# Whole-group x transfers, a new order of transfers and an earlier table load in a matmul with bias and residual

## The chip, the core and the metric

The kernel runs on one core of a Trainium2 chip. A core has five engines that work side by side, each with an instruction queue of its own: TensorE (PE) for matrix products, VectorE (DVE), ScalarE (ACT), GpSimd (POOL) and SyncE (SP). SP computes nothing here. It issues the transfers (DMAs) between the chip's main memory and the on-chip memory, and each transfer is spread over 16 DMA engines. The engines keep step by semaphores: an instruction waits until a counter has reached a value.

The metric is the device time of one execution in microseconds (us). The median of three runs before the change is 210.46 us, the lowest 210.41 and the highest 210.52.

## The reference

```python
batch, m, k, n = 16, 512, 1024, 768
# x: [16, 512, 1024], weight: [1024, 768], bias: [768], residual: [16, 512, 768], all float32
return (np.matmul(x, weight) + bias + residual).astype(np.float32)
```

The sixteen batches are one matrix of 8192 rows. x has 33.6 MB, the residual and the output 25.2 MB each, the weight 3.1 MB.

## The kernel before

The 8192 rows are cut into 8 groups of 1024 rows. Within a group each of the 128 partitions holds 8 consecutive rows, so a partition's share of x is 8 rows of 4 KB, 32 KB that lie together in main memory; its share of the residual and of the output is 24 KB that lie together. The program handles x in halves of 4 rows a partition (B = 4), that is 16 halves. "Row tile" below means the 128 rows that have the same place j (0 to 7) in all partitions.

One large tile, `data`, holds everything that SP moves: four slots for residuals, which also become the output (the sum is formed in place and stored from there), and two slots for x, used by even and odd groups in turn. Two exceptions: the weight is first loaded over the fourth residual slot and what follows it, and the residual of group 7 lies in the x slot of the even groups (`r_home`).

The steps of one half:

- ACT (lines 122 to 132) waits for the half of x and casts it to bf16 in two pieces (`cast_x`, line 114), then copies half of the transposed blocks from `tq` to their place in `xt` (`move_blocks`, line 119, 8 copies). The semaphore of the first halves is `xa`, that of the second halves `xb`; each half adds 16, and the waited value rises by 16 each group. The semaphore `cast` counts the casts, four per group.
- DVE (lines 150 to 172) transposes the 32x32 blocks: `tq` from the first cast piece (line 136), `xt` directly from the second (line 142). Between those it adds the product in PSUM to the residual (`evacuate`, line 148), two row tiles at a time: those of places 0 and 2 in the second half of the same group, those of 4 and 6 in the first half of the next. Before its loop it clears `bias_rows` (line 150), waits for the bias to land (line 152) and spreads it over the partitions (line 153). Nothing on DVE's queue passes that wait.
- PE (lines 260 to 284) waits for the weight's cast (`wc`), then does for each half 4 row tiles of 8 pairs of matmuls, 128x512 and 128x256.
- POOL (lines 182 to 204) casts the weight in two parts, then adds the bias in place to two row tiles at a time (line 190).

SP walks through `ORDER` (line 216). Each name is one transfer: `x3a` and `x3b` the halves of group 3, `r3` its residual, `st3` its store, `st4+` the store of groups 4 and 5 together, `st7a` to `st7c` parts of the last store, `w0` and `w1` the halves of the weight. Waits in front of a transfer hold up all that stand behind it on SP: x of group 2 and later waits until the group two before it is cast (its slot is then free); a transfer of the kind `xa`, `xb` or `r` waits until the one before it of that kind has landed; r4 to r6 wait until the store four groups before has landed, r7 until group 6 is cast; a store waits until POOL has added the bias, the last one until DVE is done; the bias waits until DVE has cleared its tile.

```python
ORDER = ("x0a w0 w1 bias x0b r0 x1a x1b r1 x2a x2b r2 x3a x3b r3 x4a x4b st0 st1 r4 x5a x5b r5 "
         "st2 x6a x6b r6 x7a x7b r7 st3 st4+ st6 st7a st7b st7c ").split()
```

ACT's program also holds an instruction that the source doesn't show: a load of its function table, which the compiler places in front of the first cast, inside the loop over groups.

Of the kernel before, what the change touches and what calls it, by code (L numbers as in the profile page):

```python
# [7 lines left out]
FP32 = mybir.dt.float32  # L8
BF16 = mybir.dt.bfloat16
U32 = mybir.dt.uint32  # L10
P = 128
Q = 32
G = 8
B = 4

ORDER = ("x0a w0 w1 bias x0b r0 x1a x1b r1 x2a x2b r2 x3a x3b r3 x4a x4b st0 st1 r4 x5a x5b r5 "
         "st2 x6a x6b r6 x7a x7b r7 st3 st4+ st6 st7a st7b st7c ").split()
PARTS = {"": (0, 8), "a": (0, 4), "b": (4, 8)}
LAST_PARTS = {"a": (0, 4), "b": (4, 6), "c": (6, 8)}


@with_exitstack
def kernel(
    ctx: ExitStack,
    tc: tile.TileContext,
    x: bass.AP,
    weight: bass.AP,
    bias: bass.AP,
    residual: bass.AP,
    out: bass.AP,  # L30
):
    nc = tc.nc
    with tc.tile_critical(name="all", no_gpsimd_drain=True), ExitStack() as es:  # L33
        emit(nc, es, x, weight, bias, residual, out)


def emit(nc, es, x, weight, bias, residual, out):
    x2d = x.flatten_outer_dims()
    res2d = residual.flatten_outer_dims()
    out2d = out.flatten_outer_dims()  # L40
    M, K = x2d.shape
    N = weight.shape[1]
    R = K // P
    KH = K // 2
    n_sub = M // P
    n_grp = n_sub // G
    n_bat = n_sub // B
    chunks = [(0, 512), (512, N - 512)]
    sp, act, dve, pool, pe = nc.sync, nc.scalar, nc.vector, nc.gpsimd, nc.tensor

    def sbuf(name, shape, dtype):
        return es.enter_context(nc.sbuf_tensor(name, shape, dtype))

    R_SLOT, X_SLOT = G * N, G * K
    X1, X0 = 4 * R_SLOT, 4 * R_SLOT + X_SLOT
# [2 lines left out]
    bias_rows = sbuf("bias_rows", [P, N], FP32)  # L58
    bias_bc = sbuf("bias_bc", [P, N], FP32)
    xb = sbuf("xb", [P, 2, B, R // 2, 2 * Q, 2], BF16)  # L60
    tq = sbuf("tq", [P, B, R // 2, 2, Q], U32)
    xt = sbuf("xt", [P, 2, B, R // 2, P], U32)
    po = es.enter_context(nc.psum_tensor("po", [P, 4, 1024], FP32))
# [3 lines left out]
    def sem(name):  # L67
        if name not in sems:
            sems[name] = es.enter_context(nc.semaphore(name))
        return sems[name]  # L70

    def wait(eng, name, value):
        eng.wait_ge(sem(name), value)
# [14 lines left out]
    def group(ap, g):  # L88
        return ap[g * G * P:(g + 1) * G * P, :].rearrange("(p j) k -> p j k", p=P)

    def span(start, size):
        return data[:, start:start + size] if isinstance(start, int) else data[:, bass.ds(start, size)]

    def x_half(g, half):
        return span(X0 - (g % 2) * X_SLOT + half * (B * K), B * K).rearrange("p (t k) -> p t k", k=K)

    def r_home(g):

        return (g % 4) * R_SLOT + ((g + 1) // n_grp) * (X0 - 3 * R_SLOT)

    def r_rows(start, j, n):
        return span(start + j * N, n * N).rearrange("p (j n) -> p j n", n=N)
# [7 lines left out]


    def cast_x(g, half, c):
        part = x_half(g, half)[:, :, c * KH:(c + 1) * KH]
        act.copy(out=xb[:, c],  # L114
                 in_=part.rearrange("p t (a j r) -> p t j a r", j=R // 2, r=2)).then_inc(sem("cast"), 1)

    def move_blocks(half, q):
        for m in range(P // Q):
            act.copy(out=xt[q * Q:(q + 1) * Q, half, :, :, m * Q:(m + 1) * Q],  # L119
                     in_=tq[m * Q:(m + 1) * Q, :, :, q]).then_inc(sem("mv"), 1)  # L120

    xa, xo = Rising(act, "xa", 16, 16), Rising(act, "xb", 16, 16)
    tm, tqs = Rising(act, "tm", 1, 1), Rising(act, "tq", 1, 1)
    with act.Fori(0, n_grp) as g:  # L124
        for half, loaded in ((0, xa), (1, xo)):
            loaded.wait()
            cast_x(g, half, 0)
            tm.wait()
            cast_x(g, half, 1)
            tqs.wait()  # L130
            for q in (0, 1):
                move_blocks(half, q)
# [49 lines left out]
    for h in (0, 1):  # L182
        part = slice(h * (R // 2), (h + 1) * (R // 2))
# [24 lines left out]
    def load_into(name):  # L208

        before = landed.get(name, 0)  # L210
        landed[name] = before + 16
        if before:
            wait(sp, name, before)
        return name

    for name in ORDER:
        into = name
        if name == "bias":
            wait(sp, "ev", EV0)
            src, dst = bias[None, :].to_broadcast((P // Q, N)), bias_rows[0:P:Q, :]  # L220
        elif name[0] == "w":
            k0 = int(name[1]) * (R // 2)
            src, dst = w_rows[:, k0:k0 + R // 2, :], w_stage[:, k0:k0 + R // 2, :]
        elif name[0] == "x":
            g, part = int(name[1]), name[2:]
            j0, j1 = PARTS[part]
            if g > 1 and part == "a":
                wait(sp, "cast", 2 * (2 * g - 2))
            if g == 3 and part == "a":
                wait(sp, "wc", 2)  # L230
            into = load_into(name[0] + part)
            src, dst = group(x2d, g)[:, j0:j1, :], x_half(g, j0 // B)
        elif name[0] == "r":
            g = int(name[1])
            if g == n_grp - 1:
                wait(sp, "cast", 2 * (2 * g))
            elif g > 3:
                wait(sp, f"st{g - 4}", 16)
            into = load_into("r")
            src, dst = group(res2d, g), r_rows(r_home(g), 0, G)  # L240
        else:
            g, part = int(name[2]), name[3:]
            n = 2 if part == "+" else 1
            j0, j1 = (LAST_PARTS if g == n_grp - 1 else PARTS)[part.strip("+")]
            end = (g + n - 1) * G + j1
            if end == n_sub:
                wait(sp, "ev", ev_end)
            else:
                wait(sp, "add", added[end - 1])
            src, dst = r_rows(r_home(g), j0, j1 - j0), group(out2d, g)[:, j0:j1, :]  # L250
            if n > 1:
                src = span(r_home(g), n * R_SLOT).rearrange("p (g k) -> p g k", g=n)
                dst = out2d[g * G * P:(g + n) * G * P, :].rearrange(
                    "(g p j) n -> p g (j n)", g=n, p=P)
            if g > 2:
                into, stored = "st", stored + 16
        sp.dma_start(out=dst, in_=src).then_inc(sem(into), 16)
# [4 lines left out]
    with pe.Fori(0, n_bat) as b:  # L262
        mv.wait()
        tm.wait()
        for i in range(B):
# [4 lines left out]
            for k in range(R):  # L270
                lhsT = words[:, k // 2, k % 2, :]
                for c, (n0, nl) in enumerate(chunks):
                    dst, rhs = po[:, i, n0:n0 + nl], w_sb[:, k, n0:n0 + nl]
                    if c == 0:
                        ins = pe.matmul(dst, lhsT=lhsT, rhs=rhs, start=(k == 0), stop=(k == R - 1))  # L275
                    else:
                        ins = pe.add_instruction(mybir.InstMatmult(  # L277
                            name=nc.get_next_instruction_name(),
# [34 lines left out]
```

## Time and profile before

| | before |
|---|---|
| median of 3 runs | 210.46 us (210.41 to 210.52) |
| the profiled execution, its own time | 210.49 us |
| its span, first to last instruction | 208.7 us |
| PE busy | 170.1 us, 82% of the span |
| DVE busy | 166.3 us, 80% |
| ACT busy | 154.0 us, 74% |
| POOL busy | 115.5 us, 55% |
| DMA packets' time, share of 16 engines' span | 97.9% |
| bytes moved | 87.05 MB, mean 417 GB/s |

The span is what the profile shows; the profiled execution's own time is 1.8 us longer, since it includes what lies before the first and after the last instruction. "Share of 16 engines' span" adds the time of all DMA packets and divides by 16 times the span. A packet is one contiguous run that a DMA engine moves, or the 4 bytes with which it raises a semaphore at the end of its part of a transfer. The trace holds a record of each packet: start, duration and bytes.

By the trace's packet records the first packet starts at 2.2 us. Fifteen of the sixteen DMA engines end between 205.2 and 205.8 us and one ends at 207.2 us with the same bytes (5.44 MB).

### The profile page before, as it was taken

Reading aid. Unit: us, or ns where it says so; the run is one execution under the profiler, and the core shown is the slowest. Engines: PE = TensorE matmul, PEld = TensorE weight load, DVE = VectorE, ACT = ScalarE, POOL = GpSimd, SP = SyncE. Lnnn points to the kernel's source line nnn. Section 1 sums busy time; section 2 is a strip of 40 time slices with the busy share of each in tenths; the row PEclk is TensorE's granted clock in tenths of the full one; section 3 lists DMA queues with packets and bytes.
Section 4 is the critical chain, followed back from the end, with each engine's and each line's share of the span. In section 5 each row is a group of like instructions: output and inputs, shape, how many; then the busy total and the mean of one; then the engine's idle time right before and its main releaser. Section 6 shows DMA issues by size and latency. Waiting matters only on the chain.

```text
span 208.7 us, 2836 instructions
## 1 busy us (share of the span) xinstructions
PE 170.1 (82%) x1024; PEld 50.5 (24%) x512; DVE 166.3 (80%) x180; ACT 154.0 (74%) x168; POOL 115.5 (55%) x38
## 2 busy tenths in 40 slices
PE   0000399999999999999999999999999999999800
PEld 0000123332332233323322333233323222223200
DVE  1009686899989998999899989998999899983500
ACT  0365997697989799979997998889897989720000
POOL 0055002918484757566665757484839392999700
PEclk9999999999999999999999999999999999999965
DMA  6999999999999999999999999999999999999993
GB/s 207 433 427 455 414 427 446 454 404 408 449 415 436 443 414 436 443 447 391 443 443 405 451 410 447 413 436 430 429 429 446 429 405 452 443 424 410 436 415 139
DMA packets 5176, 87.05 MB, mean 417 GB/s; under 512 B 564, under 2 KB 564, under 8 KB 824
## 3 DMA queue, kind: packets, MB, share of 16 engines
q1 hardware_dynamic: 5176, 87.05, 97.9%
HBM read 61.88 MB, written 25.17 MB: 417 GB/s over the span
## 4 chain that ended last, share of the span: by engine, by line
DVE 30%; ACT 22%; issue 16%; DMA 15%; PE 10%; ACTq 1%; DVEq 1%; SPq 0%
DVE xt L142 17%; DMA data<-in_x_dram 15%; ACT xt L119 12%; ACT xb L114 8%; DVE tq L136 7%; PE po L275 7%; DVE data L148 6%; PE po L277 3%; ACT L114 2%; DVEq L84 1%; ACTq L84 0%; ACTq L114 0%; ACTq L124 0%; DVEq L148 0%; SPq L308 0%
## 5 line engine op out<-in xcount | busy, mean ns | idle before, releaser
L275 PE MATMUL po<-w_sb,xt 128*128 128x512 bf16 x512 | 169.2, 383 | 27.1 <-DVE xt L142 24.1
L190 POOL TENSOR_TENSOR data<-data,bias_bc 128x1536 f32<-128x1536 f32 x32 | 109.8, 3454 | 68.9 <-DVE data L148 68.7
L277 PE MATMUL po<-w_sb,xt 128*128 128x256 bf16 x512 | 140.6, 275 | 0.0
L119 ACT COPY xt<-tq 32x512 uint32<-32x512 uint32 x128 | 78.9, 617 | 20.1 <-DVE tq L136 17.3
L142 DVE STREAM_TRANSPOSE xt<-xb 32x512 uint32<-32x512 uint32 x128 | 90.2, 704 | 2.7 <-ACT xb L114 0.7
L275 PEld LDWEIGHTS po<-w_sb,xt 128*128 x512 | 50.5, 99 | 146.3 <-issue 144.4
L148 DVE TENSOR_TENSOR data<-po,data 128x1536 f32 (+2 forms) x33 | 56.0, 1709 | 12.4 <-PE po L277 11.9
L114 ACT CAST xb<-data 128x2048 bf16 x32 | 64.9, 2077 | 0.3
L136 DVE STREAM_TRANSPOSE tq<-xb 128x1024 uint32<-128x1024 uint32 x16 | 19.8, 1235 | 1.6 <-ACT xb L114 1.6
L114 ACT ACT_TABLE_LOAD x8 | 10.3, 1283 | 9.8 <-DMA data<-in_x_dram 9.6
L185 POOL CAST w_sb<-data 128x3072 bf16<-128x3072 f32 x2 | 5.5, 2744 | 12.8 <-DMA data<-in_weight_dram 12.8
L153 DVE LOAD_MASK_SELECT bias_bc<-bias_rows x1 | 0.0, 14 | 14.0 <-DMA bias_rows<-in_bias_dram 14.0
L150 DVE MEMSET bias_rows<- 128x768 f32 x1 | 0.7, 698 | 1.2 <-SPq L33 1.2
L153 DVE STREAM_SHUFFLE bias_bc<-bias_rows 128x768 f32<-128x768 f32 x1 | 1.0, 1005 | 0.0
L297 POOL MEMSET const-float32-0.0<- 128x1 f32 x1 | 0.1, 98 | 0.2 <-issue 0.2
L297 POOL MEMSET const-bfloat16-1.0<- 128x1 bf16 x1 | 0.1, 101 | 0.0
L297 POOL MEMSET const-uint8-127<- 128x1 uint8 x1 | 0.1, 101 | 0.0
L297 POOL MEMSET const-float32-1.0<- 128x1 f32 x1 | 0.1, 98 | 0.0
## 6 DMA issues: line engine op xcount, KB each, us to landing
data<-in_x_dram SPq DMA_DIRECT2D x16, 2048.0 KB, 17.1
data<-in_residual_dram SPq DMA_DIRECT2D x8, 3072.0 KB, 17.1
out_dram<-data SPq DMA_DIRECT2D x5, 3072.0 KB, 23.9
out_dram<-data SPq DMA_DIRECT2D x1, 6144.0 KB, 31.1
data<-in_weight_dram SPq DMA_DIRECT2D x2, 1536.0 KB, 12.3
out_dram<-data SPq DMA_DIRECT2D x1, 1536.0 KB, 10.1
out_dram<-data SPq DMA_DIRECT2D x2, 768.0 KB, 8.6
bias_rows<-in_bias_dram SPq DMA_DIRECT2D x1, 12.0 KB
```

The lines of the kernel that those rows point to most:

```text
L84: self.eng.reg_add(self.reg, self.reg, self.step)
L114: act.copy(out=xb[:, c], in_=part.rearrange("p t (a j r) -> p t j a r", j=R // 2, r=2)).then_inc(sem("cast"), 1)
L119: act.copy(out=xt[q * Q:(q + 1) * Q, half, :, :, m * Q:(m + 1) * Q], in_=tq[m * Q:(m + 1) * Q, :, :, q]).then_inc(sem("mv"), 1)
L136: dve.transpose(out=tq[:], in_=xb_words(0)).then_inc(sem("tq"), 1)
L142: ins = dve.transpose(out=xt[q * Q:(q + 1) * Q, half, :, :, m * Q:(m + 1) * Q], in_=words[m * Q:(m + 1) * Q])
L148: dve.tensor_add(out=rt, in0=po[:, j % 4:j % 4 + n, :N], in1=rt).then_inc(sem("ev"), 1)
L150: dve.memset(bias_rows[:], 0.0).then_inc(sem("ev"), EV0)
L153: dve.stream_shuffle(out=bias_bc[:], in_=bias_rows[:], mask=[0] * 32).then_inc(sem("bb"), 1)
L185: pool.tensor_copy(out=w_sb[:, part, :], in_=w_stage[:, part, :]).then_inc(sem("wc"), 1)
L190: pool.tensor_add(out=rt, in0=rt, in1=bias_bc[:, None, :].to_broadcast((P, 2, N))).then_inc(sem("add"), 1)
L275: ins = pe.matmul(dst, lhsT=lhsT, rhs=rhs, start=(k == 0), stop=(k == R - 1))
L277: ins = pe.add_instruction(mybir.InstMatmult(name=nc.get_next_instruction_name(), ins=[pe.lower_ap(rhs), pe.lower_ap(lhsT, for_matmul_weig ...
```

## The change

Three things change. x of groups 2 to 7 is loaded by one transfer a group, 32 KB in each partition, where there were two of 16 KB; both halves are then covered by `xa`. So that ACT's wait on `xb` holds no more from group 2 on, SP adds 96 to `xb` once, in front of the load of group 3. The order of transfers is new: the bias goes second, before the weight; st2 goes between x6 and x7, x7 before r6, and r7 behind st3. And ACT copies one constant column into a new small tile `warm` ahead of its loop; in the changed program the table load stands in front of that copy and no longer inside the loop.

```diff
-ORDER = ("x0a w0 w1 bias x0b r0 x1a x1b r1 x2a x2b r2 x3a x3b r3 x4a x4b st0 st1 r4 x5a x5b r5 "
-         "st2 x6a x6b r6 x7a x7b r7 st3 st4+ st6 st7a st7b st7c ").split()
+ORDER = ("x0a bias w0 w1 x0b r0 x1a x1b r1 x2 r2 x3 r3 x4 st0 "
+         "st1 r4 x5 r5 x6 st2 x7 r6 st3 r7 st4+ st6 st7a st7b st7c").split()
 PARTS = {"": (0, 8), "a": (0, 4), "b": (4, 8)}
+WHOLE = 2
...
+    warm = sbuf("warm", [P, 1], FP32)
...
-    def x_half(g, half):
-        return span(X0 - (g % 2) * X_SLOT + half * (B * K), B * K).rearrange("p (t k) -> p t k", k=K)
+    def x_rows(g, j, n):
+        return span(X0 - (g % 2) * X_SLOT + j * K, n * K).rearrange("p (t k) -> p t k", k=K)
...
     def cast_x(g, half, c):
-        part = x_half(g, half)[:, :, c * KH:(c + 1) * KH]
+        part = x_rows(g, half * B, B)[:, :, c * KH:(c + 1) * KH]
...
+    act.copy(out=warm[:], in_=nc.const_aps.tensor(0.0, [P, 1], FP32))
     xa, xo = Rising(act, "xa", 16, 16), Rising(act, "xb", 16, 16)
     tm, tqs = Rising(act, "tm", 1, 1), Rising(act, "tq", 1, 1)
     with act.Fori(0, n_grp) as g:
...
             j0, j1 = PARTS[part]
-            if g > 1 and part == "a":
+            if g > 1:
                 wait(sp, "cast", 2 * (2 * g - 2))
-            if g == 3 and part == "a":
+            if g == 3:
                 wait(sp, "wc", 2)
-            into = load_into(name[0] + part)
-            src, dst = group(x2d, g)[:, j0:j1, :], x_half(g, j0 // B)
+                sp.sem_inc(sem("xb"), 16 * (n_grp - WHOLE))
+            into = load_into("xb" if part == "b" else "xa")
+            src, dst = group(x2d, g)[:, j0:j1, :], x_rows(g, j0, j1 - j0)
```

## The prediction, made before the changed kernel ran

> **What bounds the kernel now.** I read the page's slices and DMA queue first, since four engines are busy 74 to 98% and a share alone doesn't say which of them ends last.
>
> ```profile
> DMA  6999999999999999999999999999999999999993
> DMA packets 5176, 87.05 MB, mean 417 GB/s; under 512 B 564, under 2 KB 564, under 8 KB 824
> q1 hardware_dynamic: 5176, 87.05, 97.9%
> ```
>
> Of 40 slices only the first and the last are not full. Then the windows: one group in the middle (21.4 us), the last stretch of compute, and the end.
>
> ```profile
> 45.00:66.40 21.40, 20.97 (x131) 6.26 (x64) 20.54 (x23) 19.28 (x22) 13.74 (x4) 1.00 1.01 430
> 170.00:198.00 28.00, 26.81 (x164) 7.92 (x81) 21.40 (x22) 12.60 (x16) 22.51 (x7) 1.00 1.00 428
> 198.00:208.70 10.70, 0.00 (x0) 0.00 (x0) 0.24 (x1) 0.00 (x0) 0.00 (x0) 0.57 0.66 280
> ```
>
> The columns are length, busy time of PE, weight load, DVE, ACT and POOL, the granted clock, the DMA share and GB/s. In a group's 21.4 us PE works 20.97 and the DMA share is 1.01 (packets overlap by a few ns). But from 198 us on no engine but DVE does anything, for 0.24 us, and the DMAs go on. So compute has finished and the transfers set the end. The timeline of SP's queue shows how much they lag:
>
> ```profile
> 8.31 12.84 SPq L257 DMA_DIRECT2D data<-in_x_dram  x2
> 28.11 0.33 SPq L257 DMA_DIRECT2D data<-in_residual_dram  x1
> 33.07 5.16 SPq L257 DMA_DIRECT2D data<-in_x_dram  x2
> 45.21 0.33 SPq L257 DMA_DIRECT2D data<-in_residual_dram  x1
> 50.17 5.15 SPq L257 DMA_DIRECT2D data<-in_x_dram  x2
> 62.30 0.33 SPq L257 DMA_DIRECT2D data<-in_residual_dram  x1
> ...
> 156.81 41.79 SPq L257 DMA_DIRECT2D out_dram<-data  x6
> ```
>
> SP issues r1 at 28.11 when r0 has landed, r2 at 45.21 when r1 has, r3 at 62.30: 17.1 us for two x halves and one residual. The last store is issued at 198.6 (156.81 + 41.79), and by the packet records the last DMA engine ends at 207.2: 8.6 us of work were queued. The chain of waits, which gives DVE 30% and ACT 22%, follows the last store's wait into compute and does not see that queue. What counts is therefore the DMA engines' own work, on the one that ends last: it ends 1.5 us behind the others, because its 24 KB store packets beside compute take about 945 ns against 910.
>
> **The change part by part.** *Larger runs.* The packet records of that last engine give, from one packet's start to the next, 610.9 ns for 16 KB of x and 912.1 ns for 24 KB of residual, both beside compute. So 8 KB more cost 301.2 ns, and 32 KB come to 912.1 + 301.2 = 1213.3 ns, an estimate, where two halves take 2 x 610.9 = 1221.8. That saves 8.5 ns a pair. Each DMA engine moves 8 partitions, in 6 groups: 48 pairs, 0.41 us. Each transfer also ends with a 4-byte packet of 6 ns; six fewer save 0.04 us. No trace shows a 32 KB packet. If none of its stretch beside compute were per packet (16 KB take 607 ns without compute, 24 KB 908), it would be 1209 + 2 x 3.9 = 1217, a gain of 0.24 us; if it stayed at 1209, 0.61 us. A loss can't be excluded: at the stretch of that engine's stores (945/908) it is 1258 ns, 1.7 us more. I take 1213, the line through the two nearest rows of the same kind.
>
> The issue of one transfer instead of two (0.33 us each on SP) lies in SP's idle time. What it removes is an early landing: half 0 of a group can start when 4 MB have landed, 4.9 us later than its own 2 MB. That lies beside DMA work as long as the queue never runs dry.
>
> *The order.* I walked down the new order with 4.9 us for an x half, 9.75 for a whole group, 7.3 for a residual or a store (17.1 above), 3.7 for half a weight. Up to r1 the sum of bytes is as before: x0b 21.1, r0 28.1, x1a 33.1, r1 45.2. Then x2 lands at 55.0, r2 62.3, x3 72.0, r3 79.3, x4 89.1, st0 96.4, st1 103.7, r4 111.0, x5 120.8, r5 128.1, x6 137.8, st2 145.1, x7 154.9, r6 162.2, st3 169.5, r7 176.8, st4+ 191.4. Each SP wait on a landing ends while at least one residual, store or x stands behind it in the queue: 7.3 us of work, against 1.3 us from an issue to its first packet (x0a: issue 0.95, packet 2.2). The waits on compute must end before the landing they stand with. The tightest is x4 (group 2 cast): x2 lands at 55.0 and the two halves' casts end about 13.5 us later, as in the groups before (57.0 to 70.8), at 68.5 against 72.0. x7 wants group 5 cast: 120.8 + 13.5 = 134.3 against 137.8. r7 wants group 6 cast, about 156, against 162.2. POOL's adds of group 1 end at 76.0 now, for st1 (x4 keeps the queue until 89), those of group 3 at 118.8, for st3, which stands at 145, and those of group 5 at 161.6, for st4+ at 163. So moving st2, x7, r6, st3 and r7 costs nothing; uncovered, each us of a late issue beyond 6 (7.3 - 1.3) is one us of the end.
>
> *The bias second, the table load ahead.*
>
> ```profile
> L153 DVE LOAD_MASK_SELECT bias_bc<-bias_rows x1 | 0.0, 14 | 14.0 <-DMA bias_rows<-in_bias_dram 14.0
> L114 ACT ACT_TABLE_LOAD x8 | 10.3, 1283 | 9.8 <-DMA data<-in_x_dram 9.6
> ```
>
> DVE stood 14.0 us for the bias, until 15.87, with its transposes behind it and PE behind those (first matmul 24.09). The bias now follows x0a (landed 8.3), so DVE is free at about 9.5, earlier than its first cast (10.6). Next late is the weight: POOL's second cast starts at 15.95 and takes 2.75, so PE starts at about 19, 5.1 earlier. SP now waits at the bias for DVE's clearing (1.18 + 0.70 = 1.88) with the weight's two issues (1.40 before) and all others behind it: they go out at about 2.6, while x0a keeps the DMA engines until 8.0. Little of the 5.1 us stays: x1a lands at 33.07 as before and ACT starts group 1 1.28 us sooner, for the table load; x2 whole at 55.0, x5 at 120.8 (its cast began at 121.23, so PE's group 5 begins about a us sooner than before), r6 at 162.2 (wanted about 162). Seven of eight table loads (1.28 us each) go, but in a middle group the loop that closes is PE's batch and DVE's transposes and additions, not ACT, which had 1.2 us idle. Compute should end about 0.8 us earlier, at 197.4, under a queue that lasts to 206.8. The stretched stores stop with compute (the last at 196.2): one fewer, 0.03 us.
>
> *Sum:* -0.41 - 0.04 - 0.03 = -0.48 us. The profiled execution took 210.49 for its span of 208.7, the median of the runs is 210.46: 210.46 - 0.48 = 209.98.
>
> **The rivals.** *Nothing gained (0.13):* the DMA engines are held by the memory's rate, and what a packet costs is hidden under it; the time stays at 210.46. For it: reads beside compute stretch by 4 ns a packet, so something else than the packet limits them at times. Against: without compute the packets are equal to the ns, and the last engine works without a gap. The page DMA: Bandwidth & Descriptors of the Trainium skill, section Where 436 GB/s comes from, has main memory bind at about 358 GB/s, which would make this rival certain. The trace disagrees, with 430 in the window of a group.
>
> *More gained (0.17):* the last engine's stores recover with compute. If all 5.1 us of the earlier start last to the end, five store packets of st6 take 908 instead of 945: 0.19 us, and 1209 for 32 KB brings 0.61: 210.46 - 0.84 = 209.6. Against it: the landings of x1a, x5 and r6.
>
> *Slower (0.08):* 32 KB runs move at a lower rate, in x2 to x7 on the last engine. Break-even is at 1222 + 0.8 ns a packet, slower by more than 0.2% (0.42 us, what I take as the least that a measurement of this kernel tells from none) beyond 1232; at 1258 it is 48 x 36 ns - 0.04 = 1.7 us, 212.2. For it: nothing here is longer than 24 KB. Against: 12, 16 and 24 KB lie on one line without compute (456, 607, 908).
>
> *Compute sets the end (0.03):* if the chain of waits were right, the 5.1 us of PE's start would come off: 205.4. Against it are the 8.6 us queued at the last issue.
>
> *Each transfer pays its own start (0.02):* six transfers fewer at 1.3 us (first issue to first packet) give 7.6 us: 202.9. The packet records show 6 ns between transfers. The same page of the Trainium skill, section Anatomy of one DMA — SWDGE (gpsimd) path, fits a fixed 2.0 us to each DMA of another queue kind; by it six fewer would be 12 us. The trace shows such a cost only at the two ends of the kernel.
>
> **How the numbers follow.** The forecast has 0.57, its own range 209.75 to 210.25. The time is that of the forecast, 209.98. The range reaches to most of the larger gain and past no gain, 209.5 to 210.6; left out are the slower case, the two large gains and 0.07 for the ends of the others. Faster by over 0.2% means below 210.04: 0.31 of the forecast's 0.57 (its centre lies 0.06 us below that line), 0.16 of the larger gain, 0.05 of the two large ones: 0.52. Slower: 0.08 and 0.02 for a dry queue that the walk missed: 0.10. The rest, 0.38, is within 0.2%.
>
> **What would show it.** 32 KB packets near 1213 ns; packets fewer by 768 + 96, so 4312; all slices between the ends still 9; r2 issued near 45.2 and r3 near 62.3; PE's first matmul near 19; one table load; the end of compute well before the last packet. A slice below 9 in the middle, or 32 KB packets beyond 1222 ns, would make the prediction wrong.

## The result, and the profile after

The changed kernel takes 211.09 us (median of 10 runs, 210.38 to 211.51); the kernel before, run beside it, 210.44 (10 runs, 210.27 to 210.65). The ratio is 1.003, with a 95% interval of 1.0022 to 1.0038: slower by 0.65 us, where 0.48 us less was forecast. Its profiled execution took 210.89 us with a span of 209.1, 0.40 more than the profiled execution before. The runs also scatter more: 1.1 us from the fastest to the slowest, against 0.4. The traces below therefore explain 0.40 of the 0.65 us; the rest lies in runs that left no trace.

The page of the changed kernel first, the lines that answer to those of before:

```profile
DMA  6999999999999999999999999999999999999991
DMA packets 4312, 87.05 MB, mean 416 GB/s; under 512 B 468, under 2 KB 468, under 8 KB 728
q1 hardware_dynamic: 4312, 87.05, 97.4%
```

The packets are fewer by 864, as counted, and their time is 97.4% of 209.1 us where it was 97.9% of 208.7, some 0.7 us less a DMA engine. About 0.2 of that is no saving: the records of packets that follow each other overlap by 3 to 4 ns, and each engine has 54 packets fewer. The queue is full in every slice but the first and the last. The timeline of SP's queue (start, length, transfers):

```profile
28.05 0.33 SPq L261 DMA_DIRECT2D data<-in_residual_dram  x1
33.01 0.33 SPq L261 DMA_DIRECT2D data<-in_x_dram  x1
45.13 0.33 SPq L261 DMA_DIRECT2D data<-in_residual_dram  x1
54.85 0.33 SPq L261 DMA_DIRECT2D data<-in_x_dram  x1
62.16 0.33 SPq L261 DMA_DIRECT2D data<-in_residual_dram  x1
...
162.43 0.33 SPq L261 DMA_DIRECT2D data<-in_residual_dram  x1
162.81 36.80 SPq L261 DMA_DIRECT2D out_dram<-data  x5
```

r2 and r3 go out at 45.13 and 62.16, x3 at 54.85, when x2 has landed: the walk down the order came out to a few tenths of a us. The last store is issued at 199.6 (162.81 + 36.80). The windows of the changed kernel (length, PE, weight load, DVE, ACT, POOL, granted clock, DMA share, GB/s) and the lines of the early steps:

```profile
130.00:141.00 11.00, 9.05 (x47) 2.42 (x23) 10.83 (x13) 9.26 (x11) 6.84 (x2) 0.84 0.98 422
170.00:198.00 28.00, 27.41 (x168) 8.21 (x84) 21.66 (x23) 13.55 (x18) 23.18 (x7) 1.00 1.00 427
198.00:209.10 11.10, 0.25 (x2) 0.00 (x0) 0.96 (x1) 0.00 (x0) 0.36 (x1) 0.70 0.60 255
```

```profile
L156 DVE LOAD_MASK_SELECT bias_bc<-bias_rows x1 | 0.0, 14 | 6.7 <-DMA bias_rows<-in_bias_dram 6.7
L124 ACT ACT_TABLE_LOAD x1 | 1.3, 1283 | 0.9 <-SPq L34 0.9
```

The bias and the table load did what was foreseen: DVE waits 6.7 us for the bias instead of 14.0, one table load is left of eight, and PE's first matmul starts at 19.56. Compute nevertheless ends later, not earlier (DVE's last addition ends at 199.3, before at 198.2): whole x5 lands at 120.6 and leaves a gap of 1.95 us in PE's work at 130.8, and from 134.1 to 137.5 us the granted clock is 0.5 (0.84 in the window above). That is still under the queue.

So where did the time go? The page can't tell, since it averages 16 DMA engines. The packet records can: the times at which the engines finish their last packet (us), and the longest late packet of r7 (its time above the usual 0.912). Packet times from here on count from the zero of the timelines. Those ahead of the result lie 0.23 us later: on the timelines' axis the first packet of the kernel before starts at 1.97 us and the last ends at 206.99.

```
                         15 engines, mean   last engine   r7's latest packet
before                        205.21           206.99          none
changed                       204.66           207.39          0.84 at 175.0
changed, second trace         204.78           207.40          0.91 at 174.9
```

On fifteen engines the saving is there: 0.55 and 0.43 us. The sixteenth, which was 1.8 us behind before, is 2.7 and 2.6 us behind, and it ends the kernel: 207.39 - 206.99 = 0.40 us, the whole difference of the two profiled executions. One packet of r7 on that engine took about twice its time. Followed from start to end in the second trace, that engine spends 0.42 us less than before on x2 to x7 and 0.89 more on r7; all else adds up to 0.06 less.

### The profile page after: what moved, and what is told of

Its sections match the earlier page's. It is cut to its first block, busy times and chain, and to the rows that moved or that the text cites. A ratio compares the mean times of both kernels' runs of the same rounds, so it can differ in the third digit from the quotient of the medians.

```text
span 209.1 us, 2808 instructions
## 1 busy us (share of the span) xinstructions
PE 171.4 (82%) x1008; PEld 50.8 (24%) x512; DVE 166.6 (80%) x180; ACT 144.7 (69%) x162; POOL 115.5 (55%) x38
## 3 DMA queue, kind: packets, MB, share of 16 engines
q1 hardware_dynamic: 4312, 87.05, 97.4%
## 4 chain that ended last, share of the span: by engine, by line
DMA 57%; PE 16%; DVE 12%; issue 5%; ACT 4%; DVEq 0%; SPq 0%; ACTq 0%
DMA data<-in_x_dram 45%; DMA out_dram<-data 11%; PE po L279 10%; DVE xt L145 7%; PE po L281 5%; DVE data L151 3%; ACT xb L116 2%; ACT xt L121 2%; DVE tq L139 2%; SPq L261 0%; DVEq L86 0%; ACTq L86 0%; ACTq L116 0%; DVEq L151 0%; DVEq L158 0%
## 5 line engine op out<-in xcount | busy, mean ns | idle before, releaser
L279 PE MATMUL po<-w_sb,xt 128*128 128x512 bf16 x496 | 166.8, 386 | 26.0 <-POOL w_sb L188 19.6
```

## The experiments

Each was timed in five rounds beside the kernel before. The runs fall into four sets (e1 to e4, a2 to e7, e8 to e10, e11 and e12), in which the medians of before are 210.32, 210.46, 210.35 and 210.56.

| kernel | what it has | median, us | ratio to before (95%) |
|---|---|---|---|
| e1_whole | whole x alone | 211.65 | 1.0068 (1.0049 to 1.0087) |
| e2_tail | late order alone | 210.76 | 1.0021 (1.0012 to 1.003) |
| e3_head | bias and table load alone | 210.32 | 0.9999 (0.999 to 1.0007) |
| e4_oldtail | changed, old late order | 211.3 | 1.0056 (1.0036 to 1.0076) |
| a2_again | changed kernel again | 210.96 | 1.0024 (1.0015 to 1.0033) |
| e5_split | changed, 16 KB runs, same waits | 211.01 | 1.0027 (1.0016 to 1.0037) |
| e6_early | changed, x5 and x6 earlier | 211.34 | 1.0036 (1.0022 to 1.0049) |
| e7_r7late | e4 with r7 behind st3 | 210.94 | 1.0019 (1.0011 to 1.0028) |
| e8_r7only | before, r7 behind st3 | 210.72 | 1.002 (1.0009 to 1.003) |
| e9_single | e2 with st4 and st5 apart | 210.91 | 1.0026 (1.0016 to 1.0036) |
| e10_mixed | whole x2 to x4, old late order | 210.12 | 0.999 (0.9981 to 0.9999) |
| e11_all_but_x6 | whole x but x6, old late order | 210.28 | 0.9989 (0.998 to 0.9998) |
| e12_r7later | before, r7 behind st4 | 211.25 | 1.0031 (1.0021 to 1.0041) |

**One part at a time.** The change has three parts; these four take them apart. What was expected of each stands behind the edits, in their order.

```diff
# e1_whole: the changed kernel without the warm copy, and
-ORDER = "x0a bias w0 w1 ... r4 x5 r5 x6 st2 x7 r6 st3 r7 st4+ ..."
+ORDER = "x0a w0 w1 bias ... r4 x5 r5 st2 x6 r6 x7 r7 st3 st4+ ..."
# e2_tail: the kernel before, and
-ORDER = "... r5 st2 x6a x6b r6 x7a x7b r7 st3 st4+ ..."
+ORDER = "... r5 x6a x6b st2 x7a x7b r6 st3 r7 st4+ ..."
# e3_head: the kernel before with the warm copy, and
-ORDER = "x0a w0 w1 bias x0b ..."
+ORDER = "x0a bias w0 w1 x0b ..."
# e4_oldtail: the changed kernel, and
-ORDER = "... r5 x6 st2 x7 r6 st3 r7 st4+ ..."
+ORDER = "... r5 st2 x6 r6 x7 r7 st3 st4+ ..."
```

> Only the whole-group x loads, in the old order, with the bias behind the weight and the table load inside the loop. Theory A (the late loads r6 and r7, now among the stores, hold up the one DMA engine that ends last): faster than before by 0.3 to 0.5 us, 209.95 to 210.15. Theory B (the 32 KB packets themselves make that engine lag): slower by about 0.6 us, near 211.1. Theory C (the earlier start of compute and the bubbles it leaves shift what runs beside the stores): as A, 210.0.

> Only the order of the late transfers is new (x6 st2 x7 r6 st3 r7), x in halves, bias and table load as before. A: slower by 0.9 to 1.3 us, 211.3 to 211.8, with single packets of r6 or r7 stalled by 0.3 us or more on the engine that ends last. B and C: as before, 210.3 to 210.6.

> Only the bias second and the table load ahead of the loop. A and B: as before within 0.15 us, 210.3 to 210.6, with PE's first matmul near 19 us. C: slower by 0.6 us or more, above 211.0.

> The changed kernel with the old order of the late transfers (r5 st2 x6 r6 x7 r7 st3); whole x, bias second and the table load ahead stay. A: faster than before by 0.3 to 0.5 us, 209.95 to 210.15. B: near 211.1, as the changed kernel. C: near 211.1 too.

Theory C is out: the early part changes nothing (e3). The late order alone costs 0.44 us (e2), half of what A expected, and a packet of r7 is late by 0.34 us. Whole x in the old order costs far more, 1.33 us (e1), against A, and e4, at 211.3, speaks against A too. The trace of e1 shows why, and it is not the packets' rate. The timelines of e1_whole show the issues of x7, r7 and the last three stores on SP's queue, and DVE's last addition:

```profile
145.22 0.33 SPq L260 DMA_DIRECT2D data<-in_x_dram  x1
159.86 0.33 SPq L260 DMA_DIRECT2D data<-in_residual_dram  x1
...
198.56 5.19 SPq L260 DMA_DIRECT2D out_dram<-data  x3
```

```profile
202.44 0.96 DVE L150 TENSOR_TENSOR data<-po,data 128x768 f32<-128x768 f32 x1 [1.57 <-PE po L280]
```

Group 6 can't be cast before x6 has landed whole, at 145.2; its casts end at 159.8, and only then may r7 go out (159.86). In the old order r7 stands right behind x7, whose packets end between 160.6 and 161.7 us on the sixteen engines: the queue is all but empty, and by the packet records r7's first packet takes 0.96 to 2.25 us instead of 0.91 on fifteen of them. A gap of 3.6 us in PE's work and 3.4 us at a granted clock of 0.5 behind it move the end of compute to 203.4 and the last store's issue to 203.75 (198.56 + 5.19). All sixteen engines then end within 0.8 us, 207.2 to 208.0: hardly any backlog is left, and compute sets the end. The changed kernel's order, with st3 ahead of r7, covers that wait, so e1 exaggerates what whole loads cost in the changed kernel. In e4 r7 goes out late as well (158.71). Near 166 to 170 us r7's last packets are slow on all engines of e1 and, on some by over 1 us, of e4; that I can't explain.

**Packets or landing.** The first expectation behind these edits is that of a2_again, the changed kernel itself.

```diff
# e5_split: x2 to x7 as two transfers issued at the same place; ACT and SP wait for both
-ORDER = "... x2 r2 x3 ..."
+ORDER = "... x2a x2b r2 x3a x3b ..."
...
+    with act.Fori(0, WHOLE) as g:
+        act_group(g, (xa,), (xo,))
+    with act.Fori(WHOLE, n_grp) as g:
+        act_group(g, (xa, xo), ())
...
+                wait(sp, "xb", 16 * g)
...
# e6_early: the changed kernel, and
-ORDER = "... x4 st0 st1 r4 x5 r5 x6 st2 x7 ..."
+ORDER = "... x4 st0 x5 r4 st1 x6 r5 st2 x7 ..."
# e7_r7late: e4_oldtail, and
-ORDER = "... x7 r7 st3 st4+ ..."
+ORDER = "... x7 st3 r7 st4+ ..."
```

> The changed kernel once more, for a second trace and as the measure of the three runs beside it. All theories: 210.9 to 211.3. If the loss sits in single late packets, the trace shows some of them on the engine that ends last, in the last packets of a load that stands in front of a store.

> The changed kernel with each whole load of x cut into two transfers of 16 KB a partition that are issued at the same place; ACT and SP still wait for both, so compute and issues keep the changed kernel's times. Theory P (the 32 KB packets cost the time): 210.3 to 210.6, the time of before with the new order's share, and no slow packets at the end of x4. Theory G (the later landing of x, and what it does to compute and to the issues, costs the time): 211.4 to 211.7, the changed kernel plus the 0.45 us that the shorter packets take.

> The changed kernel with x5 and x6 moved forward (x4 st0 x5 r4 st1 x6 r5 st2 x7 r6 st3), so that x5 lands near 106 us instead of 121 and PE has no gap near 130 to 145; packets stay at 32 KB. Theory G: 210.0 to 210.4, since the gap in compute goes. Theory P: 210.9 to 211.3 as the changed kernel.

> The kernel of e4_oldtail (changed kernel, old order of the late transfers) with st3 put in front of r7, so that r7's wait for group 6's casts no longer stands where the queue ends. If a nearly empty queue at r7 made e4 slow (its first packets of r7 took 1.4 to 1.7 us): 210.6 to 211.0. If it is something else about the long packets: near 211.3 as e4.

a2_again came out as expected, with its late packet in r7. e5 lies between the two theories, at the changed kernel's time. (Its x2 goes out at 37.91 us instead of 33.01, since it also waits for x1b; the later loads go out within 0.6 us of the changed kernel's.) In the packet records its 15 engines end at 205.24 on the mean (a2_again: 204.78), so the long packets do save their 0.45 us there; its last engine ends at 207.60 (207.40), 0.2 later. The long runs cost nothing by their rate; in the changed kernel part of their saving is lost on one engine. e6, which expected a gain from closing the gap at x5, is no faster: r5 now stands in front of a store as r6 and r7 do, three of their packets are late by 0.46, 0.66 and 0.61 us, and the last engine is 3.4 us behind. It closes the gap near 131 us, but another of 2.8 us opens at 163.1, so e6 alone does not decide on G. What speaks against G, as far as x5 goes, is e11 (below): it keeps a gap of 2.2 us at 130.7 and is faster than before. e7 is better than e4 by moving r7 off the empty end of the queue, as expected, but it keeps the late group 6, and its windows show that compute sets its end:

```profile
198.00:204.00 6.00, 4.66 (x29) 1.27 (x13) 3.17 (x3) 0.00 (x0) 4.22 (x2) 1.00 0.71 298
204.00:209.20 5.20, 0.00 (x0) 0.00 (x0) 0.00 (x0) 0.00 (x0) 0.00 (x0) 0.85 0.65 266
```

From 198 to 204 us the DMA share is 0.71 while PE, DVE and POOL still work: the transfers wait for compute.

**r7 alone, and the price of a packet.** Again the expectations stand in the order of the edits.

```diff
# e8_r7only: the kernel before, and
-ORDER = "... x7a x7b r7 st3 st4+ ..."
+ORDER = "... x7a x7b st3 r7 st4+ ..."
# e9_single: e2_tail, and
-ORDER = "... st3 r7 st4+ st6 ..."
+ORDER = "... st3 r7 st4 st5 st6 ..."
# e10_mixed: the changed kernel, x5 to x7 in halves (xb raised by 48), and
+ORDER = "... x4 st0 st1 r4 x5a x5b r5 st2 x6a x6b r6 x7a x7b r7 st3 st4+ ..."
# e11_all_but_x6: the changed kernel, x6 in halves (xb raised by 64, and 16 at r7), and
+ORDER = "... x4 st0 st1 r4 x5 r5 st2 x6a x6b r6 x7 r7 st3 st4+ ..."
# e12_r7later: the kernel before, and
-ORDER = "... x7a x7b r7 st3 st4+ st6 ..."
+ORDER = "... x7a x7b st3 st4 r7 st5 st6 ..."
```

> The kernel before with one change: r7 goes behind st3, so it stands between two stores; x in halves, all else as before. Theory R (the late load r7 between two stores stalls on the DMA engine that ends last): slower by 0.3 to 0.6 us, 210.7 to 211.05, with a packet of r7 near 175 us that takes 0.3 us or more too long. Theory M (the other moves, st2 behind x6 and r6 behind x7, make e2_tail's loss): as before, 210.3 to 210.6.

> The kernel of e2_tail with the store of groups 4 and 5 as two transfers, st4 and st5, behind r7. If r7's stall comes from the double store of 6 MB that follows it: 210.3 to 210.6, without a stalled packet near 175 us. If it comes from any store that follows r7 while the last engine lags: 210.7 to 211.0 as e2_tail.

> Whole loads of x for groups 2 to 4 alone, halves for 5 to 7, the bias second and the table load ahead, and the old order of the late transfers. The saving of 24 pairs of packets and three semaphore packets is 0.22 us. If what costs time in the changed kernel are the late loads between stores and the late landings of x5 to x7: 210.1 to 210.35, a little faster than before. If 32 KB packets cost by themselves (the slow last packets of x4): 210.4 to 210.8.

> Whole loads for all groups from 2 but group 6, whose halves stay, in the old order of the late transfers, with the bias second and the table load ahead. If the price per packet carries over (40 pairs of packets at 8.5 ns and five semaphore packets at 6) and only r7's place and the late landing of a whole x6 cost time: before minus 0.37 us, 210.0 to 210.15, and faster than before. If 32 KB packets in x5 and x7 cost by themselves: 210.4 or more.

> The kernel of e8_r7only with st4 and st5 apart and r7 behind st4 instead of behind st3, so that it moves near 177 to 184 us. If a load that stands between stores stalls at its end on the lagging engine: a packet of 0.3 us or more too long near 182 us, 210.7 to 211.1. If the stall belongs to the time near 175 us, whatever moves then: none near 182 us, and 210.3 to 210.6.

e8 settles the order: r7 behind st3, and nothing else, costs 0.37 us (0.19 to 0.63 by its interval), with a packet of r7 late by 0.43 us at 175.0. That is nearly all that e2 costs, so M falls. Its kept trace is one of its faster runs (210.53) and shows less: st4+ takes 0.17 us less than before on that engine, and it ends 0.04 us later than before. e9 shows that the double store behind r7 is not needed for it (0.40 us late). e12 moves the late packet with r7, to 183.0, 0.80 us late: it belongs to r7's place and not to the time. e12 took 211.25, above its range. In it the late r7 also holds up DVE (1.74 us), which stands in the trace but under the queue.

e10 and e11 bear out the price of a packet. The old order with whole x2 to x4 gains 0.23 us where 0.22 were worked out from 8.5 and 6 ns; all groups but 6 gain 0.28 where 0.37 were, and at 210.28 miss the range of 210.0 to 210.15. Both are faster than the changed kernel, and than the kernel before by little more than the noise (by the intervals at least 0.02 and 0.04 us). The page of e11 shows the count that goes with it:

```profile
DMA  5999999999999999999999999999999999999993
DMA packets 4456, 87.05 MB, mean 418 GB/s; under 512 B 484, under 2 KB 484, under 8 KB 744
```

What r7 does to the last engine, in all traces where the queue was not empty when it began (packet records; "behind" is the last engine's final packet of a transfer against the median of all):

```
kernel           r7 stands    behind, before r7   behind, after r7   late packet of r7
e11_all_but_x6   behind x7        0.79 us             0.79 us           none
before           behind x7        0.83                0.83              none
e10_mixed        behind x7        0.87                0.86              none
e3_head          behind x7        0.93                0.92              none
e8_r7only        behind st3       0.96                1.39              0.43 us
a2_again         behind st3       1.14                1.98              0.91
e7_r7late        behind st3       1.16                1.75              0.62
e2_tail          behind st3       1.17                1.51              0.34
e9_single        behind st3       1.17                1.55              0.40
e5_split         behind st3       1.24                1.85              0.64
changed          behind st3       1.25                2.11              0.84
e12_r7later      behind st4       1.52                2.31              0.80
e6_early         behind st3       2.20                2.81              0.61
```

In every trace with a store ahead of r7 a packet of it is late on that engine, and in none of these with x7 ahead. In the changed kernel its late packet runs from 174.95 to 176.70, and the fifteen others end r7 and begin st4+ between 175.15 and 175.84: it is late while the others turn from loading to storing. Whether the place between stores does it, or the larger distance that a store adds beforehand, these runs don't separate. Neither can be the whole of it. A load in front of a store, but behind an x, can be late too: r5 and r6 in e6 (0.46 us at a distance of 0.78, 0.66 at 1.47), r6 in the changed kernel (0.33 us at 0.77, but 0.08 in its second trace), and r7 in e4, by 0.73 us at a distance of some 0.7, though that engine's queue was not empty. Yet at distances of 0.79 to 0.93 r7 behind x7 is not late in four traces above.

## Why the prediction was wrong, step by step

- *What bounds the kernel* was right: the DMA queue, and of the 16 engines the last one. The rival that compute sets the end was wrong for the changed kernel. It is right for e1 and e7, where whole x6 lands late, behind st2, and compute ends at 203.4 and 203.7. The lag between queue and compute was read 0.23 us too large (8.4 us were queued at the last issue, not 8.6; 1.0 us pass from issue to first packet, not 1.3), which changes nothing in the argument.
- *Larger runs:* right in mechanism and size. 32 KB packets follow each other at 1213 to 1214 ns, 1213.3 were worked out; the fifteen engines end 0.55 and 0.43 us earlier in two traces, and the sixteenth, too, spends 0.42 us less on x2 to x7. The slower rival (packets at a lower rate) is out, and so is a cost or gain of 1.3 us or more per transfer.
- *The order:* this is the step that failed: "So moving st2, x7, r6, st3 and r7 costs nothing". It asked only whether the queue runs dry, and that it didn't. It did not ask which loads then stand between stores. Moving r7 behind st3 costs 0.37 us by itself (e8). In the changed kernel one late packet of r7 costs the last engine 0.84 and 0.91 us, which undoes the saving of 0.4 to 0.5 and adds 0.4. That r7's place is the cause there too is carried over from e8 and e12: no run puts r7 alone back in the changed kernel, and e4, which puts the whole late order back, has slow packets of another kind. Why the packet is later with whole loads (0.84 and 0.91 us) than with halves (0.34 to 0.43; 0.64 with the changed kernel's waits) is open.
- *The walk* through landings was right to 0.3 us (x5 120.6 for 120.8, r7's issue 162.43 for 162.2). That r7's wait for group 6 stands safely was right only for the new order; in the old one whole x6 makes it late (e1, e4).
- *The bias and the table load at nothing:* right (e3: ratio 0.9999). PE now waits for the weight, as foreseen. "Compute should end about 0.8 us earlier" was wrong, 1.0 later: the gap at x5 and the slower clock behind it weren't in the sum. e5 has such a gap without the slow clock, and its compute ends at 198.2, as before. It cost nothing, since the queue covered it.
- *Main memory's rate:* the rival in which nothing is gained fell, since the fifteen engines gained. The Trainium skill (DMA: Bandwidth & Descriptors, section Where 436 GB/s comes from) has main memory bind at about 358 GB/s a core, worked out as half of a memory stack's rate. It does not bind in this kernel, which runs on one core: the windows of the changed kernel beside compute have 422 and 427 GB/s. No run here has a second core at work.

## What to carry to other kernels

When the transfers set the end, look at the DMA engine that ends last and not at their mean: what all sixteen save is worth nothing if the sixteenth loses it elsewhere. When transfers are put in a new order, ask of each load not only whether the queue stays full but what stands on both sides of it; here a packet of a load between two stores was late by 0.3 to 0.9 us on the last engine. A larger transfer is also a later landing: take it where what waits for it has slack (here every group but 6, in the old order, which beat both kernels).

## What the runs showed of the hardware that was not expected

- One DMA engine of 16 takes about 945 ns for most 24 KB stores beside compute, the others about 910. Its last one, after compute, takes 912 to 916 in the traces, and its loads are mostly as fast as the others'. That compute is the reason isn't shown. The records don't name the engine; in all traces but those of e1 and e7 such an engine ended last, 1.7 to 3.4 us behind the mean of the others.
- A queue that is nearly empty when a load begins makes its first packets cost 0.96 to 2.25 us instead of 0.91 (e1, at 161 us); at the kernel's start the first packets of 16 KB take 0.75 to 1.5 us instead of 0.61.
- In the changed kernel PE's granted clock was 0.5 for 3.4 us, in both traces, 0.5 to 1.3 us after a gap of 2 us in PE's work; in the kernel before, without such a gap, it stayed at 1.00. The gap alone doesn't decide it: gaps of 2.3 us (e5), 2.8 (e6) and 3.6 (e4) were followed by no slower clock.
